# The place of the seventh product between two pairs of column blocks in a hybrid decoder layer

## The chip, the cores and the metric

The kernel runs on one core of one Trainium2 chip. The metric is device time in microseconds (us) for one execution. Three executions of the kernel before took 1405.05, 1405.37 and 1412.27 us; the median is 1405.37 us.

## The reference, cut to what matters

One layer of a decoder with two parallel branches, in float32, on 1024 tokens of width 1024:

```
mod   = silu(c) @ ada_w + ada_b                      # shift, scale, gate
h     = rms_norm(x) * (1 + scale) + shift            # 1024 x 1024
proj  = h @ w_in                                     # 1024 x 11296
gm_u, gm_v, gm_z, ssm_z, xbc, dt_raw, g_a, g_b = split(proj)
y_a   = spatial_gating(gelu(gm_u), gelu(gm_v)) * silu(gm_z)
xbc   = silu(causal_depthwise_conv(xbc))             # 4 taps
y_b   = group_norm((ssd_scan(xbc, dt) + skip) * silu(ssm_z))
merged = sigmoid(g_a) * (y_a @ w_proj_a) + sigmoid(g_b) * (y_b @ w_proj_b)
out   = rms_norm(x + gate * (merged @ w_out))
```

The change concerns `h @ w_in` alone, the widest product.

## The kernel before, in words

Each matrix product is made in float32r from a high and a low part of either operand (high times high, high times low, low times high), and the large ones by a Strassen-Winograd scheme, in which seven products of half-size blocks stand for eight. The stages are: modulation and normalisation (to about 70 us in the profile), the **wide stage** `h @ w_in` (to about 922 us), the state-space scan with `y_a @ w_proj_a` beside it, `y_b @ w_proj_b`, and the output product.

In the wide stage the blocks of `h` stay in on-chip memory. The columns of `w_in` come in blocks of 128, and two blocks make a pair. There are 43 pairs: four of v (v0 to v6), then pairs for the convolution (cb0 to cb7 and x0 to x7) mixed with uz0 to uz7, with z0 to z7 and with seven pairs of gates (g2 to g14). `pair` (L580) makes one pair. Its seven products are called p1, p5, p6, p3, p2, p7 and p4; each is 12 matmuls of 128x512 (`product`, L570). They go to three accumulators in PSUM:

- `px` takes p1. ScalarE copies it to the first half of the tile c1 (L600). Then p6 is added in the same bank, and ScalarE copies the sum to the second half of c1 (L611). Then p7 is added, and VectorE adds px and the saved p5 into the second half of the tile c2 (L622). Last p4 is added, and ScalarE copies px to the first half of c2 (L630).
- `py` takes p5, which ScalarE saves (L606); then p3 is added, and VectorE adds it to c1 (L614).
- `pz` takes p2, which VectorE adds to the first half of c1 (L595).

When c1 is whole, `done1` treats the first block, and after p4 `done2` treats the second: a convolution is one ScalarE pass (L916), three VectorE passes (L918), a SiLU (L920) and a store to DRAM from ScalarE's queue (L93); z and g are one ScalarE pass and a store; u is a GELU, a VectorE product and a store.

The seventh product, p4, isn't made within its own pair. It is put on the list `pending` (L636) and made inside the next pair. Three pairs have nothing pending when they begin, since they are the first or follow a pair made whole: v0, cb0 and g12. The other 40 take over a p4.

What sets the order: TensorE's instructions are pinned (`pin`, which keeps them in the order of the program), and so are the loads on the SP queue. The instructions of ScalarE and VectorE in this stage are mostly not pinned. A scheduler orders them ahead of the run, and gives those issued through `out` (L588) high priority. Each engine then runs its list in order. After each product `run_tasks` (L495) issues the side tasks that have come due; a task's due time counts products.

The tiles c1, c2, the convolution's result ac, the tiles vm and ya of the gating branch, and the short-lived tiles of side tasks (ag and gacc for the output gate, wog for gated weights) all come from one ring of 1024-column tiles, tag w4, with six buffers (`wide`, L164). The writer of a new tile waits until an earlier user of the buffer is done, a store's landing included.

A line in the profile of an instruction issued through `out` is L590, of a matmul in the wide stage L574, of a high part's cast L522. The name `xx<-t4h,p4x2h` tells of a matmul that adds to px of an x pair, here p4 of the pair x2.

Of the kernel before, what the change touches and what calls it, by code (L numbers as in the profile page):

```python
# [35 lines left out]
def hybrid_kernel(  # L36
# [7 lines left out]
    V, A, G, PE = nc.vector, nc.scalar, nc.gpsimd, nc.tensor  # L44
    ctx.enter_context(nc.allow_non_contiguous_dma(reason="small parameter vectors"))

    x, out = x[0], out[0]
# [116 lines left out]
    def wide(name, dt=F32):  # L164
        return w4[0].tile([P, S], dt, name=name, tag="w4", bufs=w4[1])
# [315 lines left out]
    def bank(name):  # L481

        if pairs_done:
            pairs_done.append(name)
            if len(pairs_done) % 4 == 2:
                return psum.tile([P, 512], F32, name=name, tag="px", bufs=2)
        return psum.tile([P, 512], F32, name=name, tag="bk", bufs=6)
# [7 lines left out]
    def run_tasks():  # L495
        slot[0] += 1
        due = [t for t in tasks if t[0] <= slot[0]]
        for t in due:
            tasks.remove(t)
            t[1](*t[2])  # L500
# [69 lines left out]
    def product(ps, l, bn, first=True):  # L570
        (lh, ll), (rh, rl) = l, bop[bn]
        for n, (lw, r) in enumerate(((lh, rh), (lh, rl), (ll, rh))):
            for k in range(4):
                pin(PE.matmul(ps, lw[:, k * P : (k + 1) * P], r[k], start=first and n + k == 0,  # L574
                              stop=n == 2 and k == 3, skip_group_check=not first))
        run_tasks()
# [3 lines left out]
    def pair(name, ops, done1, done2, after=None, whole=False):  # L580

        keep = pin if name in first_c1 and not p2r else lambda i: i
        after = after or (lambda n: None)

        def out(f, *a):  # L588
            with tc.high_priority():
                keep(f(*a))  # L590

        def p2():
            pz = bank(f"z{name}")
            product(pz, ops["p2"], "b21")
            out(V.tensor_add, c1[:, 0:512], c1[:, 0:512], pz)  # L595

        px = psum.tile([P, 512], F32, name=f"x{name}", tag="px", bufs=2)
        product(px, ops["p1"], "b11")
        c1 = first_c1.pop(name) if name in first_c1 else wide(f"c1{name}")
        out(A.copy, c1[:, 0:512], px)  # L600
        after(0)
        py = bank(f"y{name}")
        product(py, ops["p5"], "t1")
        c2 = wide(f"c2{name}") if p2r else None
        p5 = c2[:, 512:1024] if p2r else gm.tile([P, 512], F32, name=f"p5{name}", tag="p5")
        out(A.copy, p5, py)  # L606
        after(1)
        if pending:
            pending.pop()()
        product(px, ops["p6"], "t2", False)  # L610
        out(A.copy, c1[:, 512:1024], px)  # L611
        after(2)
        product(py, ops["p3"], "b22", False)
        out(V.tensor_add, c1[:, 512:1024], c1[:, 512:1024], py)  # L614
        after(3)
        if not whole:
            p2()
            after(4)
            done1(c1)
        product(px, ops["p7"], "t3", False)  # L620
        c2 = c2 or wide(f"c2{name}")
        out(V.tensor_add, c2[:, 512:1024], p5, px)  # L622
        after(4 if whole else 5)
        if whole:
            p2()
            done1(c1)

        def p4():
            product(px, ops["p4"], "t4", False)
            out(A.copy, c2[:, 0:512], px)  # L630
            done2(c2)

        if whole:
            p4()
        else:
            pending.append(p4)  # L636
# [603 lines left out]
    ops = pair_weights(*todo[0][:3], pinned=True)  # L1240
# [4 lines left out]
    for n, (name, _, _, d1, d2, g) in enumerate(todo):  # L1245
# [30 lines left out]
        if n + 1 == len(todo):  # L1276
            pair(name, ops, lambda t: held.append((d1, t)), lambda t: held.append((d2, t)), beside, True)
        else:
            pair(name, ops, d1, d2, ops.get("after"), n in (3, len(jobs) - 1))
        ops = nxt if n else seconds[0]  # L1280
# [532 lines left out]
```

## Time and profile before

| what | us |
|---|---|
| median of three runs | 1405.37 |
| the profiled execution | 1407.67 |
| its span, first to last instruction | 1405.9 |
| TensorE busy in the span | 1377.1 (98%) |
| VectorE busy | 1062.4 (76%) |
| ScalarE busy | 797.0 (57%) |
| GpSimd busy | 213.0 (15%) |
| mean granted TensorE clock | 0.997 of full speed |

Times are from the span's start. In a row of the timeline the first number is the start, the second the length, then come engine, line, operation, tiles, shape and count; brackets at the end tell how long the engine was idle before and what ended the wait.

### The profile page before, as it was taken

To read this page: it belongs to the slowest core of one execution; us is meant where nothing else is said; L and a number is where in the kernel's file an instruction comes from. 1 tells how busy PE (TensorE), PEld (TensorE's weight loads), DVE (VectorE), ACT (ScalarE), POOL (GpSimd) and SP (SyncE) were. 2 spreads that over 40 slices of the span, in tenths; PEclk is the share of its full clock that TensorE was granted. 3 is DMA by queue.
4 is the path that set the end of the run, shared out by engine and by line. 5 is a ranking of instruction groups with operands and counts; after the bars stand their busy time and mean duration, and the time that the engine had idled before them with its cause. 6 is when DMAs were issued, how large, how long until landed. Compare 5 with 4: busy or idle time off the path is not lost.

```text
span 1405.9 us, 20633 instructions
## 1 busy us (share of the span) xinstructions
PE 1377.1 (98%) x7035; PEld 1139.9 (81%) x7035; DVE 1062.4 (76%) x1863; ACT 797.0 (57%) x1471; POOL 213.0 (15%) x208
## 2 busy tenths in 40 slices
PE   8999999999999999999999999999999999999997
PEld 6688888888888888888887888888888877878886
DVE  4786776777778889889788796388667767876976
ACT  5764576556656665556565555677766723322443
POOL 0000000000000011111000010038778740000001
PEclk9999999999999999999999999999999999999999
DMA  8653343343344777787675774598778749878903
GB/s 263 173 165 98 113 120 105 105 121 120 116 125 134 214 202 239 236 248 232 192 221 156 240 214 135 173 353 318 262 253 296 275 168 328 320 231 296 350 33 120
DMA packets 273150, 283.37 MB, mean 202 GB/s; under 512 B 15341, under 2 KB 223637, under 8 KB 273045
## 3 DMA queue, kind: packets, MB, share of 16 engines
q1 hardware_dynamic: 185684, 198.52, 44.4%
q10 hardware_dynamic: 87360, 83.54, 17.8%
q8 instruction: 55, 0.90, 0.3%
q14 instruction: 51, 0.41, 0.1%
HBM read 194.55 MB, written 87.46 MB: 201 GB/s over the span
## 4 chain that ended last, share of the span: by engine, by line
PE 80%; DMA 8%; DVE 5%; POOL 2%; issue 2%; ACT 1%; SPq 1%; ACTq 0%; DVEq 0%; POOLq 0%
PE xcb L574 6%; PE xuz L574 6%; PE xz L574 6%; PE xx L574 5%; PE xg L574 5%; PE x L1477 4%; PE yp L1477 4%; PE ox L1676 3%; PE yuz L574 3%; PE ycb L574 3%; PE pma L81 3%; PE xv L574 3%; PE yz L574 3%; PE yg L574 3%; PE yx L574 3%; DMA dcy<-acs_d 3%
## 5 line engine op out<-in xcount | busy, mean ns | idle before, releaser
L793 POOL TENSOR_TENSOR wog<-wog,gb 128x256 f32<-128x256 f32 x16 | 18.3, 1159 | 676.6 <-PE zz L574 413.3
L1007 ACT ACTIVATE dcy<-dcy,nacs 128x128 f32<-128x128 f32 x256 | 78.6, 388 | 14.9 <-POOL dcy L1002 14.5
L1002 POOL TENSOR_SCALAR_AFFINE_SELECT dcy<-dcy 128x1024 f32<-128x1024 f32 x32 | 35.0, 1095 | 135.7 <-ACT ea L999 132.3
L999 ACT ACTIVATE ea<-dcy 64x512 f32<-64x512 f32 x64 | 40.1, 626 | 14.2 <-DMA dcy<-acs_d 13.8
L920 ACT ACTIVATE ac<-ac 128x1024 f32<-128x1024 f32 x32 | 33.9, 1060 | 23.0 <-DVE ac L918 22.8
L81 PE MATMUL pma<-yh,wah 128*128 128x512 f32 x128 | 43.3, 419 | 0.0
L1027 DVE TENSOR_TENSOR dcy<-dcy,pc 128x1024 f32<-128x1024 f32 x32 | 39.0, 1218 | 4.8 <-PE pc L84 3.0
L81 PE MATMUL pma<-yh,wal 128*128 128x512 f32 x128 | 42.5, 413 | 0.0
L1089 POOL TENSOR_TENSOR yz<-y,sl 128x512 f32<-128x512 f32 x32 | 41.4, 1295 | 1.1
L1087 DVE TENSOR_TENSOR ym<-yn,ea 128x512 f32<-128x512 f32 (+1 forms) x32 | 19.9, 622 | 28.5 <-PE yn L81 28.3
L81 PE MATMUL pma<-yl,wah 128*128 128x512 f32 x128 | 40.1, 394 | 0.0
L1088 POOL TENSOR_TENSOR y<-y,ym 128x512 f32<-128x512 f32 (+1 forms) x32 | 36.6, 1144 | 14.4 <-DVE ym L1087 14.4
L81 PEld LDWEIGHTS yn<-sl,st 128*128 128x128 f32 x224 | 30.3, 190 | 8.3 <-issue 4.4
L81 PE MATMUL yn<-sl,st 128*128 128x128 f32 x224 | 31.6, 276 | 4.9 <-DVE st L1057 4.9
L1416 DVE SCALAR_TENSOR_TENSOR yn<-yn,par,rb 128x512 f32<-128x512 f32 x32 | 24.0, 749 | 15.7 <-DMA yn<-yb_d 15.5
L81 PE MATMUL sp<-xe,bn 128*128 128x256 f32 x112 | 32.6, 408 | 3.3 <-DVE ssq L1117 1.7
L81 PE MATMUL yi<-dcy,xd 128*64 128x128 f32 x512 | 35.7, 283 | 0.0
L918 DVE SCALAR_TENSOR_TENSOR ac<-c2x,cwt,ac 128x1023 f32<-128x1023 f32 (+2 forms) x24 | 31.2, 1300 | 5.3 <-ACT ac L916 5.1
L918 DVE SCALAR_TENSOR_TENSOR ac<-c2cb,cwt,ac 128x1023 f32<-128x1023 f32 (+2 forms) x24 | 31.1, 1296 | 4.4 <-ACT ac L916 4.3
L1691 POOL TENSOR_TENSOR r<-r,fnw 128x512 f32<-128x512 f32 x2 | 2.5, 1296 | 203.7 <-DMA out_dram<-r 203.7
L1055 POOL TENSOR_TENSOR st<-st,cd 128x256 f32<-128x256 f32 x48 | 32.1, 668 | 8.0 <-PE yn L81 5.3
L918 DVE SCALAR_TENSOR_TENSOR ac<-c1cb,cwt,ac 128x1023 f32<-128x1023 f32 (+2 forms) x24 | 31.6, 1318 | 1.3 <-ACT ac L916 1.3
(2980 smaller groups left out, 4390.9 us busy)
## 6 DMA issues: line engine op xcount, KB each, us to landing
sl<-s_d SPq DMA_DIRECT2D x32, 768.0 KB
s_d<-ac ACTq DMA_DIRECT2D x32, 512.0 KB
dcy<-acs_d SPq DMA_DIRECT2D x32, 512.0 KB
aw<-in_ada_w_dram SPq DMA_DIRECT2D x16, 512.0 KB
wbr<-in_w_proj_b_dram SPq DMA_DIRECT2D x64, 128.0 KB
wb_d<-wbb ACTq DMA_DIRECT2D x32, 256.0 KB
wb_d<-wbc ACTq DMA_DIRECT2D x32, 256.0 KB
yb_d<-yz ACTq DMA_DIRECT2D x32, 256.0 KB
```

What stands on the lines that cost most here:

```text
L81: pin(PE.matmul(acc, l, r, start=first, stop=last))
L574: pin(PE.matmul(ps, lw[:, k * P : (k + 1) * P], r[k], start=first and n + k == 0, stop=n == 2 and k == 3, skip_group_check=not first))
L918: V.scalar_tensor_tensor(ac[:, s:], cc[:, : S - s], conv_wt[:, 3 - s, i : i + 1], ac[:, s:], op0=ALU.mult, op1=ALU.add)
L920: A.activation(ac, ac, AF.Silu)
L999: A.activation(ea[hh * HD : (hh + 1) * HD], dcy.rearrange("p (j e) i l -> p e j (i l)", e=2)[hh * HD : (hh + 1) * HD, hh], AF.Exp)
L1002: G.affine_select(out=d8, in_=d8, compare_op=ALU.is_ge, fill=-1e30, base=0, pattern=[[0, 2 * HPG], [1, P]], channel_multiplier=-1)
L1007: A.activation(dcy[:, h, i, :], dcy[:, h, i, :], AF.Exp, bias=sub[:, i, h : h + 1])
L1027: V.tensor_tensor(d3, d3, pc[:, 0:256].unsqueeze(1).to_broadcast([P, HPG, 256]), op=ALU.mult)
L1088: G.tensor_add(y1[:, :, t0:], y1[:, :, t0:], m[:, :, t0:])
L1089: G.tensor_mul(yz, y1, sl[:, 4:6])
L1477: pin(PE.matmul(ps[j], a[:, v, js], r, start=first and n + k == 0, stop=n == 2 and k == KT - 1, skip_group_check=not first))
L1676: pin(PE.matmul(ps, a[:, tsl], b[:, cs], start=first and n + j == 0, stop=n == 2 and j == 3, skip_group_check=not first))
```

## The change

Within a pair, the pending p4 of the pair before was made between p5 and p6. It is now made between p6 and p3.

```
@@ pair
         out(A.copy, p5, py)
         after(1)
+        product(px, ops["p6"], "t2", False)
+        out(A.copy, c1[:, 512:1024], px)
         if pending:
             pending.pop()()
-        product(px, ops["p6"], "t2", False)
-        out(A.copy, c1[:, 512:1024], px)
         after(2)
         product(py, ops["p3"], "b22", False)
```

The order on TensorE was p1, p5, p4 of the pair before, p6, p3, p2, p7; it is p1, p5, p6, p4 of the pair before, p3, p2, p7. In the 40 pairs that take over a p4, one product instead of two stands between p1 and p6, three instead of two between p6 and p7, and three instead of two (counting p1, p5 and p6) between p7 and its own pair's p4. Two stay between p5 and p3. No product, copy, load or store is added or taken away.

More of the change, by code (lines that the diff above doesn't have):

```diff
@@ L607, in pair @@
         after(1)
+        product(px, ops["p6"], "t2", False)
+        out(A.copy, c1[:, 512:1024], px)
         if pending:
             pending.pop()()
-        product(px, ops["p6"], "t2", False)
-        out(A.copy, c1[:, 512:1024], px)
         after(2)
```

## The prediction

> **What bounds the kernel now.** I read the page's first part, then a table by stage (busy time of each engine in chosen windows), then TensorE's waits.
>
> ```profile
> span 1405.9 us, 20633 instructions
> PE 1377.1 (98%) x7035; PEld 1139.9 (81%) x7035; DVE 1062.4 (76%) x1863; ACT 797.0 (57%) x1471; POOL 213.0 (15%) x208
> ```
>
> ```profile
> core 0: us, PE busy (x) PEld busy (x) DVE busy (x) ACT busy (x) POOL busy (x), PEclk, DMA share, GB/s
> 155.00:300.00 145.00, 145.00 (x681) 121.32 (x681) 107.67 (x170) 91.25 (x144) 0.00 (x0) 1.00 0.36 110
> 300.00:480.00 180.00, 180.00 (x828) 150.23 (x827) 138.90 (x186) 111.38 (x174) 0.00 (x0) 1.00 0.46 140
> 480.00:850.00 370.00, 369.26 (x1631) 304.18 (x1630) 316.42 (x592) 214.80 (x366) 30.58 (x24) 1.00 0.72 216
> 1031.25:1034.66 3.41, 3.41 (x25) 3.08 (x25) 2.56 (x4) 1.12 (x4) 2.68 (x3) 0.50 0.88 355
> ```
>
> The first three stretches cover nearly all of the wide stage. TensorE is busy for 694.26 of their 695 us. VectorE is busy 74%, 77% and 86%. So TensorE sets the pace, and two things follow. The change can win next to nothing here, for there is hardly a wait to remove. And whatever makes TensorE wait is added to the end in full, since no other engine is holding the time.
>
> The waits of TensorE in the wide stage that concern p4, p6 and p7 are these (weight loads, PEld, in their own view):
>
> ```profile
> PE xx L574 <- DVE c2x L590: 0.6, 1, 0.6
> ```
>
> ```profile
> PEld xx L574 <- DVE c2x L590: 1.0, 1, 1.0
> PEld xz L574 <- ACT c1z L590: 0.6, 1, 0.6
> PEld xz L574 <- DVE c2z L590: 0.3, 1, 0.3
> ```
>
> **What the change moves.** p6 is added in the bank of p1, so it must wait until ScalarE has copied p1 out. Before, p5 and the foreign p4 ran meanwhile; now p5 alone does. One product is 12 matmuls; from the start of p4 in one row below to the start of p6 in another (750.97 is disturbed, so take 359.47 to 362.19) it lasts 2.72 us. The question is how late the copy is. This is the pair x2, first TensorE, then ScalarE:
>
> ```profile
> 359.47 1.07 PE L574 MATMUL xuz<-t4h,p4uz4h 128*128 128x512 f32 x4
> ...
> 362.19 1.07 PE L574 MATMUL xx<-t2h,p6x2h 128*128 128x512 f32 x4
> ```
>
> ```profile
> 360.45 0.59 ACT L590 COPY c1x<-xx 128x512 f32<-128x512 f32 x1 [1.06 <-DVE gacc L764]
> ```
>
> p6 started at 362.19, long after the copy's end at 361.04, so nobody waited. In the new order p6 wants to start at 359.47, where p4 stands now, and must wait until 361.04. That is how the whole cost is read: **copy's end minus the start of the p4 that follows p5.**
>
> The price of a stop itself is seen where p4 of x6 was held up:
>
> ```profile
> 749.30 1.07 PE L574 MATMUL yz<-t1h,p5z4l 128*128 128x512 f32 x4
> 750.97 1.20 PE L574 MATMUL xx<-t4h,p4x6h 128*128 128x512 f32 x4 [0.60 <-DVE c2x L590]
> ...
> 753.83 1.07 PE L574 MATMUL xz<-t2h,p6z4h 128*128 128x512 f32 x4
> ```
>
> From 750.97 to 753.83 are 2.86 us where an undisturbed product takes 2.72. A restart therefore costs about 0.14 us more, and I add 0.04 us for the signal from ScalarE to TensorE (the delay also seen in the other direction: below, p1 of g12 ends at 885.29 = 884.22 + 1.07, and its copy starts at 885.32). Each stop costs copy's end + 0.18 - p4's start.
>
> In most pairs the copy follows p1 at once. The pair g12, which has no p4 to take over, already has the new order, and shows what happens then:
>
> ```profile
> 884.22 1.07 PE L574 MATMUL xg<-b11h,p1g12l 128*128 128x512 f32 x4
> ...
> 886.94 1.07 PE L574 MATMUL yg<-t1h,p5g12l 128*128 128x512 f32 x4
> 887.85 1.07 PE L574 MATMUL xg<-t2h,p6g12h 128*128 128x512 f32 x4
> ```
>
> ```profile
> 885.32 0.59 ACT L590 COPY c1g<-xg 128x512 f32<-128x512 f32 x1 [1.04 <-PE xg L574]
> ```
>
> The copy is over at 885.91, p6 starts at 887.85 (0.16 us before p5's last row ends at 888.01, the usual overlap), and 1.94 us are to spare. **The new order is free wherever the copy starts less than about 1.9 us after p1's end, and costs wherever it starts later.**
>
> **First term: pairs where the copy is already too late.** I went through ScalarE's timeline pair by pair. In 11 of the 43 pairs the copy ends after the p4 that follows p5 has begun: cb2, x2, x3, x4, cb5, x5, g8, g10, cb7, z5 and x7. The first and the last of them, with x3:
>
> ```profile
> 319.59 1.07 PE L574 MATMUL xuz<-t4h,p4uz3h 128*128 128x512 f32 x4
> ...
> 439.23 1.07 PE L574 MATMUL xuz<-t4h,p4uz6h 128*128 128x512 f32 x4
> ...
> 827.98 1.09 PE L574 MATMUL xz<-t4h,p4z5h 128*128 128x512 f32 x4
> ```
>
> ```profile
> 319.62 0.59 ACT L590 COPY c1cb<-xcb 128x512 f32<-128x512 f32 x1 [1.18 <-DMA s_d<-ac]
> ...
> 439.51 0.59 ACT L590 COPY c1x<-xx 128x512 f32<-128x512 f32 x1 [1.32 <-DMA s_d<-ac]
> ...
> 828.77 0.59 ACT L590 COPY c1x<-xx 128x512 f32<-128x512 f32 x1 [0.45 <-DVE wba L830]
> ```
>
> cb2: 320.21 + 0.18 - 319.59 = 0.80. x2: 361.04 + 0.18 - 359.47 = 1.75. x3: 440.10 + 0.18 - 439.23 = 1.05. x7: 829.36 + 0.18 - 827.98 = 1.56. By the same working the other seven are 0.43, 0.65, 0.46, 0.88, 1.53, 1.68 and 1.05. The 11 sum to **11.8 us**, if each copy keeps its distance from p1.
>
> **Second term: copies that move back.** Several copies are late because c1 has no buffer in the six-deep ring: the brackets name a store's landing (s_d<-ac) or the last reading of another tile of the ring (gacc, whose pass reads ag). The freed buffer is in part the work of the p4 that is moved. For the copy of cb3 the chain can be followed back. TensorE, then ScalarE:
>
> ```profile
> 382.12 1.07 PE L574 MATMUL xx<-t4h,p4x2l 128*128 128x512 f32 x4
> ...
> 399.35 1.07 PE L574 MATMUL xuz<-t4h,p4uz5h 128*128 128x512 f32 x4
> ...
> 420.19 1.07 PE L574 MATMUL xcb<-t4h,p4cb3h 128*128 128x512 f32 x4
> ```
>
> ```profile
> 383.23 0.59 ACT L590 COPY c2x<-xx 128x512 f32<-128x512 f32 x1 [0.28 <-PE xx L574]
> 383.85 1.24 ACT L916 ACTIVATE ac<-c2x,par,cwt 128x1024 f32<-128x1024 f32 x1
> ...
> 387.92 3.19 ACT L882 ACTIVATE vm<-vm,vr 128x128 f32<-128x128 f32 x8 [1.38 <-DMA vm<-v_d]
> ...
> 391.52 1.06 ACT L920 ACTIVATE ac<-ac 128x1024 f32<-128x1024 f32 x1
> ...
> 392.61 0.52 ACTq L93 DMA_DIRECT2D s_d<-ac  x1
> ...
> 397.30 0.59 ACT L590 COPY c1cb<-xcb 128x512 f32<-128x512 f32 x1 [0.75 <-DMA s_d<-ac]
> ...
> 418.58 0.59 ACT L590 COPY c1uz<-xuz 128x512 f32<-128x512 f32 x1 [1.61 <-DVE gacc L764]
> ```
>
> p4 of x2 ends at 383.19, its second convolution begins at once, its store lands, and only then can the copy for cb3 start, 14.1 us later. The new order ends that p4 one product (2.72 us) later against p1 of cb3, and wants p6 one product earlier. The copy of cb3 has 399.35 - 397.89 = 1.46 us to spare now; moved by 2.72 it would cost 2.72 - 1.46 + 0.18 = 1.44.
>
> Five copies between 300 and 480 us wait for such a buffer: cb2, x2, cb3, uz6, x3. For each the move is bounded by 0 below, since SiLUs and stores also stand in line on ScalarE behind other work (the vm passes above, 387.92 to 391.11), which doesn't move, and by 2.72 above. For cb3, whose chain begins at once, I take the whole, 1.44. For the other four I take the middle, 1.36: it adds 1.36 each to cb2, x2 and x3, and uz6 (spare 420.19 - 419.17 = 1.02) comes to 1.36 - 1.02 + 0.18 = 0.52. Together 3 x 1.36 + 1.44 + 0.52 = **6.0 us** (0 to 11.5: 3 x 2.72 + 1.44 + 1.88).
>
> **What else moves.** The moved step issues 12 matmuls, one copy and `done2`, with its ScalarE and VectorE passes and a store on ScalarE's queue; all come one product later, the last of them in the same pair as before, and only a late buffer makes that matter, which is the second term. Side tasks due at the second of the two products are now issued ahead of `done2`; their number, and the order of the loads on the SP queue, stay. GpSimd does nothing in this stage except the gated weights (30.58 us busy of 370); nothing is moved past them. The casts of the next pair's weights keep their places: their buffers are freed one per product, and that count stays.
>
> **What is won.** p4 now has three products behind p7, p7 three behind p6. The three waits quoted above go: x6's p4 (start 750.97 where 750.21 = 750.37 - 0.16 was possible, plus 0.14: 0.9), and the two PEld waits of 0.6 and 0.3, of which the part beyond a normal load and the restart make about 0.4 and 0.2. Together **1.5 us**.
>
> **Sum.** 11.8 + 6.0 - 1.5 = +16.3 us. Against the profiled execution's own time of 1407.67 that is 1424.0; that execution is 2.3 us above the median of the runs shown, 1405.37, so the forecast for the median is 1421.7, say **1422**.
>
> **Rivals.**
>
> 1. *Not slower.* ScalarE's list is drawn up anew, with the copies at high priority. Of the 11 late copies, only cb2, x2 and x3 are held by a buffer by their rows; the other eight (8.2 us) stand behind casts and passes of ScalarE that could come after them. If all eight are drawn forward to p1's end, as in g12, and buffers don't move, there remain 0.80 + 1.75 + 1.05 - 1.5 = +2.1: 1407.5. It decides at a copy that starts 1.9 us after p1's end. For it: ScalarE is busy only 58% from 480 to 850 us. Against it: the copies already had that priority and still came late. Chance 0.20.
> 2. *The ring falls behind everywhere.* 19 copies start more than 0.4 us after p1's end for another reason than TensorE's own work; if all move by the whole 2.72, the stops are 57.2 us by the same sum, and with 1.5 won the time is 1461. Half of that move (1.36) makes 31.4 us of stops, 1435. For it: VectorE is at 86% from 480 us on. Against: a z or g copy can wait for a tile freed by `done1`, which doesn't move, and each stop lets the other engines catch up. Chance 0.18, mostly between 1432 and 1450.
> 3. *The clock falls.* After the longest wait of the scan stage the granted clock is 0.50 for 3.41 us (the fourth row of the table above):
>
> ```profile
> PE yn L81 <- DVE st L1057: 4.9, 5, 2.8
> ```
>
> With the wait of 2.8 us as the point, such a fall costs half of 3.41, 1.7 us. In the forecast only x2 comes near (1.75 + 1.36 = 3.1, less 0.14 of restart and 0.16 of overlap: 2.8 us idle), and I leave its 1.7 out. With the whole 2.72 for the five buffers cb2, x2 and x3 pass it: 11.8 + 11.5 - 1.5 + 3 x 1.7 = +26.9, 1432. Chance 0.10. The Trainium skill, on the page TensorE: Matmul & The Clock Gate, in Part 1 on the HAM clock gate, states that TensorE's clock is halved after about one idle window of 3.4 us, and that the window isn't tied to the kernel. By that rule stops shorter than 3.4 us would leave the sum at +16.3, and only the ones beyond would pay; the trace agrees on the halving and its 3.41 us, but with a wait of 2.8 us ahead of it.
> 4. *Faster by over 0.5%*, 7 us: TensorE's waits here don't add up to that, so only a lucky new order in the later stages could. Chance 0.02.
>
> The forecast's own case (1412 to 1432) has 0.50. A difference of 0.5% is about what a measurement of this kernel can tell from no change. Faster 0.02, within 0.5% 0.20, slower 0.78. The range runs from 1407, in rival 1, to 1442, two thirds of the move in rival 2.
>
> **What would show it.** In the new profile TensorE's waits should name ACT c1cb, c1x, c1z or c1g at L590 ahead of p6, 10 to 16 times, 0.4 to 3 us each; p4 and p7 should wait for nothing; the time after the wide stage should be unchanged, only later. Few such waits would speak for rival 1; such waits in nearly every pair after 300 us for rival 2; a clock below 1.00 in the wide stage for rival 3. The prediction is wrong if the wide stage grows through another wait, on py, or on weights, or if the added time arises after 922 us.

## The result, and the profile after

The changed kernel took 1420.43 us (median of six runs, 1417.38 to 1427.9), the kernel before 1405.94 us on the same occasion (median of six, 1402.67 to 1412.27). The ratio is 1.011, with a 95% interval of 1.009 to 1.0131: about 14.5 us slower. A ratio here and below is worked out from all the executions of both kernels, so it isn't the quotient of the two medians. The forecast was 1422, with a range of 1407 to 1442.

The profiled execution of the changed kernel took 1417.38 us. The first part of its page:

```profile
span 1415.6 us, 20602 instructions
PE 1380.9 (98%) x7035; PEld 1140.8 (81%) x7035; DVE 1060.7 (75%) x1863; ACT 803.3 (57%) x1471; POOL 216.9 (15%) x208
```

TensorE's busy time has hardly grown (1377.1 to 1380.9), while the span grew by 9.7 us. To find the place, I cut the wide stage of each trace into parts at the start of p1 of three pairs: v0 to cb2 ("early"), cb2 to z0 ("middle"), z0 to g12 ("late"). The rows of a window table give the stretch, its length, the busy time of TensorE, its weight loads, VectorE, ScalarE and GpSimd (instructions in brackets), the granted clock, the DMA share and GB/s. First the kernel before:

```profile
70.54:314.15 243.61, 243.54 (x1137) 201.88 (x1136) 178.61 (x315) 147.12 (x235) 1.19 (x1) 1.00 0.39 119
314.15:494.48 180.33, 180.33 (x826) 149.80 (x824) 143.59 (x205) 111.47 (x173) 0.00 (x0) 1.00 0.47 142
494.48:882.40 387.92, 387.18 (x1713) 319.74 (x1712) 320.64 (x588) 221.46 (x373) 30.58 (x24) 1.00 0.69 208
```

Then the changed one, with four short windows that are used below:

```profile
70.77:314.46 243.69, 243.65 (x1137) 201.88 (x1136) 177.99 (x315) 148.81 (x235) 1.43 (x1) 1.00 0.39 119
314.46:503.17 188.71, 182.91 (x826) 150.56 (x825) 143.32 (x204) 112.37 (x174) 0.00 (x0) 0.99 0.44 135
503.17:896.87 393.70, 389.85 (x1714) 320.57 (x1713) 320.80 (x590) 225.56 (x374) 33.60 (x24) 1.00 0.69 205
360.75:364.16 3.41, 0.64 (x3) 0.19 (x1) 2.37 (x3) 1.22 (x3) 0.00 (x0) 1.00 0.78 269
364.16:367.57 3.41, 3.01 (x7) 2.43 (x8) 1.28 (x1) 0.35 (x1) 0.00 (x0) 0.50 0.76 222
780.58:784.00 3.42, 1.31 (x7) 0.77 (x6) 3.42 (x7) 2.59 (x4) 0.00 (x0) 1.00 0.27 90
784.00:787.41 3.41, 3.41 (x10) 2.63 (x9) 3.32 (x8) 2.33 (x5) 0.00 (x0) 0.50 0.62 163
```

The early part is the same (243.61 and 243.69), though ten p4s were moved there. The middle is 8.4 us longer and the late part 5.8 us. With the rest of the stage (39.4 us in both) the wide stage went from 851.2 to 865.5 us: 14.2 us. What TensorE waited for in it:

```profile
PE xx L574 <- ACT c1x L590: 4.3, 4, 3.2
PE xcb L574 <- ACT c1cb L590: 3.3, 3, 1.2
PE xg L574 <- ACT c1g L590: 2.1, 1, 2.1
```

All three rows are matmuls that add to px and wait for a copy into c1, and all are p6. The two longest stops, on TensorE and then on ScalarE:

```profile
364.56 1.65 PE L574 MATMUL xx<-t2h,p6x2h 128*128 128x512 f32 x3 [3.17 <-ACT c1x L590]
...
783.62 1.35 PE L574 MATMUL xg<-t2h,p6g10h 128*128 128x512 f32 x3 [2.11 <-ACT c1g L590]
```

```profile
363.93 0.59 ACT L590 COPY c1x<-xx 128x512 f32<-128x512 f32 x1 [1.91 <-DVE gacc L764]
...
782.99 0.58 ACT L590 COPY c1g<-xg 128x512 f32<-128x512 f32 x1
```

p6 begins 0.04 to 0.05 us after the copy's end (364.52 and 783.57). No p4 and no p7 of the wide stage waits any more.

Counted as the delay of p6 against the usual overlap of 0.16 us, eight pairs stop: cb2 1.29, x2 3.33, x3 0.42, cb4 1.39, cb5 1.07, x5 0.53, x6 0.62 and g10 2.27; with crumbs of under 0.2 us the sum is 11.3. Eight restarts of 0.14 add 1.1. The granted clock was 0.50 twice for 3.41 us, from 364.16 and from 784.00, at the end of the two longest stops. TensorE was busy for 3.01 and 3.41 us of these two windows (rows above), and half of that is lost: 3.2. The waits of p4 and p7 that are gone are worth 1.3. The sum, 11.3 + 1.1 + 3.2 - 1.3 = 14.3, accounts for the 14.2 us.

### The profile page after: what moved, and what is told of

It reads as the page before. It is cut to its first block, busy times and chain, and to the rows that moved or that the text cites. A ratio compares the mean times of both kernels' runs of the same rounds, so it can differ in the third digit from the quotient of the medians.

```text
span 1415.6 us, 20602 instructions
## 1 busy us (share of the span) xinstructions
PE 1380.9 (98%) x7035; PEld 1140.8 (81%) x7035; DVE 1060.7 (75%) x1863; ACT 803.3 (57%) x1471; POOL 216.9 (15%) x208
## 4 chain that ended last, share of the span: by engine, by line
PE 37%; DMA 7%; DVE 4%; POOL 3%; issue 2%; ACT 2%; SPq 1%; ACTq 0%; DVEq 0%; POOLq 0%
PE x L1477 5%; PE xg L574 4%; PE yp L1477 4%; PE xz L574 3%; PE ox L1676 3%; PE pma L81 2%; DMA dcy<-acs_d 2%; PE oy L1676 2%; PE yg L574 2%; DMA yb_d<-yz 2%; PE yz L574 2%; PE xcb L574 2%; PE xx L574 1%; DMA yn<-yb_d 1%; PE zg L574 1%
## 5 line engine op out<-in xcount | busy, mean ns | idle before, releaser
L1007 ACT ACTIVATE dcy<-dcy,nacs 128x128 f32<-128x128 f32 x256 | 78.5, 388 | 16.0 <-POOL dcy L1002 14.5
L999 ACT ACTIVATE ea<-dcy 64x512 f32<-64x512 f32 x64 | 40.1, 627 | 14.2 <-DMA dcy<-acs_d 13.8
```

Of the source, the lines that this page charges most:

```text
L999: A.activation(ea[hh * HD : (hh + 1) * HD], dcy.rearrange("p (j e) i l -> p e j (i l)", e=2)[hh * HD : (hh + 1) * HD, hh], AF.Exp)
L1007: A.activation(dcy[:, h, i, :], dcy[:, h, i, :], AF.Exp, bias=sub[:, i, h : h + 1])
```

## The experiments

Each time of an experiment stands beside runs of the kernel before on the same chip. "Delay" is the delay of p6 (or p4) in the wide stage, counted as above.

**Early pairs only, and late pairs only.** The new order in the first twelve pairs, or in all the others:

```
+        new = name in early          # other kernel: name not in early
+        if pending and not new:
+            pending.pop()()
         product(px, ops["p6"], "t2", False)
         out(A.copy, c1[:, 512:1024], px)
-        if pending:
+        if pending and new:
             pending.pop()()
```

> The new order only in the first twelve pairs (v0 to uz3, ten of them with a pending p4); the other pairs keep the order of before. Theory: a moved p4 costs nothing by itself, only a late copy of p1 does; in these pairs the copy starts 0.04 to 0.14 us after p1's end, so the time is that of before, 1406 within 2 us, and TensorE names no copy of c1 ahead of p6 in them. Rival: each moved p4 costs alike, 14.5 / 40 = 0.36 us, ten of them 3.6 us: about 1409.5.

Measured: 1409.68 us beside 1407.78, ratio 1.0009 (0.9992 to 1.0026): no difference. The early part and the waits of the wide stage:

```profile
71.96:315.67 243.71, 243.65 (x1138) 201.89 (x1136) 178.00 (x315) 148.71 (x234) 1.28 (x1) 1.00 0.39 119
```

```profile
PE xz L574 <- DVE c2z L590: 1.1, 1, 1.1
PE xuz L574 <- DVE c2uz L590: 0.9, 1, 0.9
```

Ten moved p4s cost nothing: the early part took 243.61 us before, and a fixed price would have added 3.6. So the rival of a fixed price falls by the trace; the time alone, whose interval ends at 1.0026 (3.7 us), couldn't exclude it. The two waits belong to p4s in the old order, later in the stage.

> The new order only from the pair cb2 on (30 moved p4s). Theory: all of the loss is here, 1420 within 3 us, with stops ahead of p6 at much the same pairs as in the changed kernel (x2 and g10 the longest). Rival, a like cost for each moved p4: 1406 + 30 x 0.36 = 1417 (the two are hard to tell apart by this run's time alone; its trace tells).

Measured: 1426.56 beside 1407.78, ratio 1.0116 (1.0091 to 1.0141), which by its interval can't be told from that of the whole change (1.011); the median lies above the 1417 to 1423 expected. Middle and late part, and the longest wait:

```profile
314.82:503.73 188.91, 183.47 (x825) 150.57 (x824) 142.87 (x204) 112.07 (x174) 0.00 (x0) 0.99 0.45 135
503.73:896.34 392.61, 388.42 (x1714) 319.40 (x1712) 321.23 (x589) 224.89 (x374) 33.21 (x24) 1.00 0.70 206
```

```profile
PE xx L574 <- ACT c1x L590: 4.6, 4, 3.4
```

The whole loss sits from cb2 on. x2 (3.5 us of delay) and g10 (2.0) are again the longest stops.

**A tile of its own for p1's copy.** c1 takes its buffer of the ring only when p6 is copied:

```
-        c1 = first_c1.pop(name) if name in first_c1 else wide(f"c1{name}")
-        out(A.copy, c1[:, 0:512], px)
+        if name in early:             # cb0 to uz7
+            c1, p1 = None, gx.tile([P, 512], F32, name=f"p1{name}", tag="p1", bufs=2)
+        else:
+            ...
+            p1 = c1[:, 0:512]
+        out(A.copy, p1, px)
...
+        c1 = c1 or wide(f"c1{name}")
         out(A.copy, c1[:, 512:1024], px)
```

> The new order in all pairs, but in the pairs cb0 to uz7 the copy of p1 goes to a tile of its own with two buffers, outside the ring of six; c1 takes its buffer of the ring only at p6's copy, one product later. Theory: the copies of cb2, x2 and x3 are late for want of a buffer of the ring, so their stops vanish (1.29 + 3.33 + 0.42 us of delay, three restarts of 0.14, and one fall of the clock at 364 us of 1.7): about 7 us less than the changed kernel, 1413. Rival: they are late because ScalarE is busy with other work; then the stops stay within half a microsecond and the time is 1420.

Measured: 1420.0 beside 1407.78, ratio 1.0069 (1.0044 to 1.0094). Middle and late part:

```profile
315.09:495.42 180.33, 180.33 (x826) 149.80 (x824) 137.87 (x192) 109.38 (x165) 0.00 (x0) 1.00 0.43 129
495.42:895.10 399.68, 392.19 (x1714) 322.40 (x1713) 325.80 (x600) 225.69 (x378) 36.14 (x24) 0.99 0.70 208
```

In the middle part the result is as clean as can be: 180.33 us, to the hundredth that of before, with TensorE busy throughout. All stops there came from the missing buffer: at cb2, x2 and x3 directly, and at cb4, which kept its tile of the ring, by way of what the pairs ahead of it leave behind. The late part, in which nothing was changed, became 6 us longer than in the changed kernel: the stop at cb5 grew from 1.07 to 3.59 us and the clock was at 0.50 for 6.8 us behind it. So the wide stage fell by 2.4 us (865.5 to 863.1) and not by the 7 expected. The time doesn't show a fall clear of noise: its interval overlaps that of the changed kernel (1.009 to 1.0131), and the median is what the rival expected. It is the trace that refuses the rival. Why the late part grew, with no edit there, no run shows; the likely reason is how the middle part leaves buffers and lists behind.

> The new order; the copy of p1 goes to a tile of its own (one buffer) in all pairs from v2 to z7, outside the ring. To make room, two small tiles of a side task (wba and wbb) share one buffer. Theory: the ring holds up the late copies after 480 us too (cb4, cb5, x5, x6, g10), if indirectly, through the order that the scheduler gave ScalarE; all stops but small ones vanish: 1406 to 1408. Rival: after 480 us ScalarE's own line of work is the reason; the stops there stay (5.9 us of delay, five restarts, one fall of the clock, 8 us in all): 1413 to 1415.

Measured: 1419.4 beside 1407.78, ratio 1.008 (1.0056 to 1.0104). The middle part is 181.28 us, the late part 400.20, with stops at x4, cb5, z2, x5, g10, cb7 and x7. Both expected times are missed, 1406 to 1408 and 1413 to 1415. None of the seven copies waits for its tile by its row, so the ring is not what held them directly. ScalarE ahead of the stop at cb7 (copy of p1 into p1cb):

```profile
800.39 0.41 ACT L830 CAST wbc<-wbr 128x256 fp32r<-128x256 f32 x1 [1.80 <-DVE wbr L850]
800.77 0.40 ACT L830 CAST wbb<-wbr 128x256 fp32r<-128x256 f32 x1
801.09 0.58 ACT L590 COPY p1cb<-xcb 128x512 f32<-128x512 f32 x1
```

ScalarE stood idle for 1.80 us until VectorE had made the side task's sum, and the copy stood behind that cast in ScalarE's list. The theory that the ring holds up the copies after uz7 as well falls. The shared buffer of wba and wbb may have made it worse; this run can't tell.

**The side task's stores on another queue.** In the changed kernel the same shows at cb5, where a store on ScalarE's queue (ACTq) is the obstacle:

```profile
583.26 0.41 ACT L825 CAST wbc<-wbr 128x256 fp32r<-128x256 f32 x1 [2.14 <-DVE wbr L845]
584.80 0.40 ACTq L93 DMA_DIRECT2D wb_d<-wbc  x1
585.24 0.62 ACT L522 CAST p1g4h<-a11g 128x512 fp32r<-128x512 f32 x1 [1.56 <-DVE wbc L830]
585.76 0.58 ACT L590 COPY c1cb<-xcb 128x512 f32<-128x512 f32 x1
```

```
-        store(wb_d[k][:, at : at + n, :, j * P : (j + 1) * P], f32(hl))
+        G.dma_start(wb_d[k][:, at : at + n, :, j * P : (j + 1) * P], f32(hl))
```

> The new order; the stores of the weight side task (wb_d, 96 of them) are issued from GpSimd's queue instead of ScalarE's. Theory for the stops after 480 us: ScalarE's line stands still while such a store waits for VectorE's subtraction, and the copy of p1 stands behind it; freed of that, the stops at cb5, x5, x6 and g10 shrink to under 0.5 us each (from 1.07, 0.53, 0.62 and 2.27 us of delay), while those up to 480 us (cb2, x2, x3) stay: 4 to 6 us less than the changed kernel, about 1415 against a before of 1407. Rival: the ring of six is the reason there too, or ScalarE is merely full; then the stops after 480 us stay within a microsecond in sum.

Measured: 1424.0 beside 1406.64, ratio 1.0119 (1.0096 to 1.0143): no gain in time. Middle and late part:

```profile
314.54:505.98 191.44, 184.50 (x825) 151.36 (x824) 143.93 (x205) 113.28 (x174) 7.58 (x10) 0.98 0.44 134
505.98:895.34 389.36, 387.23 (x1713) 319.68 (x1712) 319.18 (x589) 224.33 (x374) 90.38 (x110) 1.00 0.68 207
```

The late part did what was expected, 389.36 instead of 393.70: x5 and x6 no longer stop, cb5 has 0.63 left, but g10 keeps 1.83. Of the 4.3 us, 1.7 are the clock, which didn't fall behind g10 this time. The copy of g10 stands behind something other than those stores, a pass of the pair z4 that waits for VectorE, and a SiLU (in the changed kernel behind the same pass, at 780.81):

```profile
779.67 1.06 ACT L926 ACTIVATE c1z<-c1z 128x1024 f32<-128x1024 f32 x1 [2.26 <-DVE c1z L590]
...
782.06 1.06 ACT L920 ACTIVATE ac<-ac 128x1024 f32<-128x1024 f32 x1
783.03 0.57 ACT L590 COPY c1g<-xg 128x512 f32<-128x512 f32 x1
```

The middle part took back 2.7 us, with cb4 at 2.06 and the clock at 0.50 for 6.8 us behind x2. The expectation of the time is a miss; that of the stops is met for x5 and x6, nearly for cb5, and not for g10.

**Both, in the new order and in the old.**

> The new order with both causes taken away: the copy of p1 in a tile of its own in the pairs cb0 to uz7, and the side task's stores on GpSimd's queue. Theory (late copies are the whole cost, and these two are why they are late): TensorE's delays ahead of p6 sum to under 3 us (11.3 in the changed kernel), and the time is within 4 us of before. Rival (something else of the new order costs time, or GpSimd's queue delays the side task): over 8 us above before.

Measured: 1410.93 beside 1406.64, ratio 1.0029 (1.0014 to 1.0044); delays 5.0 us (z0, x4, cb5, g10), more than the 3 expected; the time is 4 us above before, at the edge of what was expected.

> Control for the run with both causes taken away: the own tile for p1's copy (cb0 to uz7) and the stores on GpSimd's queue, in the order of before. If the own tile and the queue cost and win nothing by themselves, this is before, 1406 to 1408, with TensorE's delays in the wide stage under 1.5 us, and what the run with the new order had above before (1.0029 times, 4 us) is the price of the new order with its remaining stops (5.05 us of delay, 0.56 of restarts). Rival: the side task on GpSimd's queue costs those 4 us in either order; then this is 1410 to 1412 too.

Measured: 1410.18 beside 1408.23, ratio 1.0011 (0.9998 to 1.0024). The late part, in the new order and then in the old:

```profile
494.73:886.93 392.20, 387.95 (x1714) 319.50 (x1713) 325.75 (x600) 224.72 (x377) 92.38 (x114) 1.00 0.69 212
```

```profile
494.76:886.90 392.14, 388.72 (x1713) 319.14 (x1712) 325.80 (x597) 219.16 (x378) 93.41 (x113) 1.00 0.68 208
```

This is the most telling pair. With the two causes taken away the order of p4 and p6 makes no difference in the wide stage that these two traces show: 855.6 and 855.5 us, both some 4.3 above the 851.2 of before. In the old order the 4.6 us of delay stand ahead of p4, which waits for VectorE's sum into c2; in the new order 5.0 us stand ahead of p6. So the stops are other ones, and that their sums agree this closely may be chance. The control didn't have the under 1.5 us expected; which of its two edits costs that was asked next.

> The order of before, the side task's stores on GpSimd's queue, no own tile. In the control with both, the part of the wide stage from z0 to z7 took 392.1 us against 387.9 before, with stops ahead of p4. If the stores' queue costs that, it is 391 to 393 here too and the time 1.002 to 1.004 times before; if the own tile does (it sets the ring's buffers on another course up to uz7), this part is 388 to 389 here and the time that of before.

Measured: 1407.19 beside 1406.11, ratio 1.0005 (0.9991 to 1.002). The late part:

```profile
494.54:882.57 388.03, 386.95 (x1713) 319.69 (x1712) 318.64 (x589) 220.72 (x373) 93.47 (x110) 1.00 0.68 209
```

388.03 us: the queue costs nothing in the old order, so it is the own tile up to uz7, added to it, that sets the late part on another course, by about 4 us. The own tile without the queue was not run in the old order.

**Work in the two longest stops.** TensorE makes useless matmuls there, whose result nobody reads:

```
+        fill_stop = {"x2": 10, "g10": 6}.get(name, 0)
+        ...
+                pin(PE.matmul(pf, ops["p5"][0][:, 0:P], bop["t1"][0][n % 4], start=True, stop=True))
         product(px, ops["p6"], "t2", False)
```

> The new order, and in the pairs x2 and g10 TensorE makes 10 and 6 more matmuls of 128x512 between p5 and p6 into a bank that nobody reads, 2.3 and 1.4 us, which fit in the idle time that stands there (3.17 and 2.11 us). They add nothing to the result. Theory: TensorE's clock fell twice because those two idle times were long, at a cost of 1.7 us each; kept busy it doesn't fall, and the wide stage is 3.4 us shorter than in the changed kernel (865.5 us), 862. Rival: the idle time has no part in it, the falls stay, the stage is as long or longer.

Measured: 1426.47 beside 1406.64, ratio 1.0146 (1.012 to 1.0171). TensorE at x2:

```profile
361.73 2.43 PE L612 MATMUL fx<-t1h,p5x2h 128*128 128x512 f32 x10
365.09 1.21 PE L574 MATMUL xx<-t2h,p6x2h 128*128 128x512 f32 x4 [0.94 <-ACT c1x L590]
```

The clock didn't fall in the wide stage at all, so the idle time is what lowered it. (It fell at x2 in all five other traces of the new order, or of the stronger dose below, in which the copy of x2 goes to the ring: the changed kernel, the late pairs, the stores on GpSimd's queue, the copy on VectorE and the stronger dose.) But the stage was 867.1 us, not 862: other stops grew (x4 from nothing to 1.63, cb5 from 1.07 to 1.66), and what the clock gave was lost again. The expected time is a miss. The row shows another thing: p6 of x2 starts 294 us after v0 with or without 2.3 us of work ahead of it (365.09 - 71.17 = 293.92; 364.56 - 70.77 = 293.79). The copy there comes at its own time, set by the pass on ag that frees its buffer: in the changed kernel that pass (L764) waits for ag's load to land, starts at 362.61 and takes 1.28 us, and the copy follows at 363.93.

**A stronger dose.** p6 directly behind p1, in all pairs but v0:

```
+        if near:
+            product(px, ops["p6"], "t2", False)
+            out(A.copy, c1[:, 512:1024], px)
         py = bank(f"y{name}")
         product(py, ops["p5"], "t1")
```

> A stronger dose: p6 stands directly behind p1 (all pairs but v0), p5 and the foreign p4 after it. By the formula (copy's end + 0.18 us - start of the next product) even a prompt copy costs 0.04 + 0.59 + 0.18 + 0.16 = 0.97 us, in 42 pairs 41 us, and the pairs with copies up to 4 us late pay up to 2.72 us more each, 13 to 19 such pairs some 30 us: 1406 + 55 to 80 = 1460 to 1485. Rival: if the loss were a fixed price of a moved product, it would be like the changed kernel's, 1420 to 1435.

Measured: 1485.92 beside 1406.64, ratio 1.0564 (1.0533 to 1.0595), just above the upper end. A pair with a prompt copy, TensorE and ScalarE:

```profile
637.81 1.07 PE L574 MATMUL xg<-b11h,p1g4l 128*128 128x512 f32 x4
639.55 1.19 PE L574 MATMUL xg<-t2h,p6g4h 128*128 128x512 f32 x4 [0.68 <-ACT c1g L590]
```

```profile
638.91 0.58 ACT L590 COPY c1g<-xg 128x512 f32<-128x512 f32 x1 [0.28 <-PE xg L574]
```

p1 ends at 638.88, p6 would have begun 0.16 earlier and begins at 639.55: 0.83 of delay and 0.14 of restart, the 0.97 of the formula. It recurs as 0.835 or 0.836 us in 20 pairs. The formula of the prediction holds for them. The total is no proof of it: the granted clock was 0.50 in seven windows of this wide stage, which cost 9.8 us (half of TensorE's busy time in them), and the expectation had nothing for that.

**The copy on VectorE.**

```
-        out(A.copy, c1[:, 0:512], px)
+        out(V.tensor_copy, c1[:, 0:512], px)
```

> The new order, the copy of p1 made by VectorE instead of ScalarE in all pairs. If ScalarE's line is the reason after 480 us, the stops at cb5, x5, x6 and g10 shrink (3.9 to 4.5 us of delay in the kernels so far become under 2), while cb2, x2 and x3 stay late for want of a buffer: about 3 us less than the changed kernel, 1.009 times before. If the lines are late on either engine alike (VectorE is 86% busy there and waits in order too), the delays stay at 10 to 13 us and the time at 1.011 to 1.015 times before.

Measured: 1446.32 beside 1408.23, ratio 1.0274 (1.0253 to 1.0294); delays 29.0 us. Both expectations missed, on the dear side. The largest two groups of waits:

```profile
PE xcb L574 <- DVE c1cb L590: 10.1, 4, 5.1
PE xx L574 <- DVE c1x L590: 5.1, 3, 3.3
```

The granted clock was 0.50 in five windows of the wide stage, 8.1 us more. The middle part grew to 205.1 us; the likely reason, which no run tested, is that a copy that waits for a buffer now holds up VectorE's list, in which passes that free buffers stand. After 480 us x5 vanished and g10 fell to 0.37, but cb5 stayed at 1.04, x6 grew to 1.63, and z4 came new with 2.76. It doesn't settle which list is late.

**The kernel before once more.**

> The kernel before once more, for a second trace. The stages behind the wide stage took 484.2 us in its first trace and 479.4 in that of the changed kernel. Theory: that is scatter between executions and no doing of the change; this trace has 484.2 only by chance and may lie anywhere from 479 to 488, while the wide stage is 851.2 within 0.5 us. Rival: the new order shortens the later stages; then it is 484 within 1.

Measured: one run, 1406.59 us; wide stage 852.3 us, 1.1 more than in the first trace and outside the 0.5 expected, since p4 of x6 waited 1.4 us instead of 0.6; the stages behind it 1404.9 - 925.2 = 479.7 (484.2 in the first trace). Over all kernels here they took 479 to 488 us whatever the order. So the 4.8 us by which the changed kernel's trace is shorter there are scatter; the medians don't have them.

This trace shows more. ScalarE takes its instructions of the wide stage in the order of the first trace, and yet the copies of p1 don't keep their places: those of z5 and x7 started 2.86 and 3.35 us after p1's end in the first trace, 0.67 and 1.84 us in the second. The working of the prediction's first term, on the second trace, gives nine late pairs in place of 11, without z5 and x7, and 10.9 us.

## Why the prediction was right, and where its sizes were off

- **What bounds the kernel.** Right. TensorE was busy through the stage, and what stops it is added to the end: 14.2 us in the stage, 14.5 between the medians.
- **The price rule** (copy's end + 0.18 - start of the next product). Right, shown by the stronger dose at 0.97 us for a prompt copy, and by the early pairs at nothing.
- **First term, late copies that keep their distance from p1: 11.8.** Too large, and mostly after 480 us. There eight pairs were to cost 8.2 us; x4, g8, cb7, z5 and x7 didn't stop, cb5, x5, x6 and g10 did, 4.5 us of delay, 5.1 with restarts. The step that failed is that each copy keeps its place. In that part the copy stands in ScalarE's list behind casts, passes and stores that wait for VectorE, and the list was drawn up anew. At cb7, where p1 ended at 787.23 before and at 801.83 after, a cast of the side task went from behind p4's cast to ahead of it. ScalarE before, then after:

```profile
786.70 0.60 ACT L522 CAST p4cb7h<-a22cb 128x512 fp32r<-128x512 f32 x1
...
788.20 0.41 ACT L825 CAST wbc<-wbr 128x256 fp32r<-128x256 f32 x1 [0.89 <-DVE wbr L845]
...
790.72 0.58 ACT L590 COPY c1cb<-xcb 128x512 f32<-128x512 f32 x1
```

```profile
799.81 0.41 ACT L825 CAST wbc<-wbr 128x256 fp32r<-128x256 f32 x1 [1.22 <-DVE wbr L845]
...
801.11 0.61 ACT L522 CAST p4cb7h<-a22cb 128x512 fp32r<-128x512 f32 x1
...
802.57 0.58 ACT L590 COPY c1cb<-xcb 128x512 f32<-128x512 f32 x1
```

  The copy came 3.49 us after p1's end before, and 0.74 after. At cb5 and x5 the order is the same in both, and only the waits differ. And z5 and x7, 2.6 of the 8.2 us, were late in the first trace of before and not, or just not enough, in the second: one execution was too little to read them from.
- **Second term, copies that move back: 6.0.** Right that the middle part suffers from the ring of six (the own tile removes all of it, 8.4 us, 1.5 of them the clock), wrong in the pairs. cb3 was to wait for the store of the moved p4's work; it started 0.45 us after p1's end. Its buffer came from another tile, c1 of the pair uz5, freed by a VectorE product:

```profile
403.85 0.59 ACT L590 COPY c1cb<-xcb 128x512 f32<-128x512 f32 x1 [0.70 <-DVE ya L902]
```

  The prediction followed one buffer; in the changed kernel the copy got another. With both terms, and restarts counted, cb3 (1.44 forecast) and uz6 (0.52) cost nothing, cb2 1.43 (2.16 forecast) and x3 0.56 (2.41); cb4 (0 forecast) cost 1.53 and x2 3.47 (3.11). So in the middle part the stops were 7.0 where the two terms had 9.6. Over the whole stage the two terms were 17.8, the stops measured 12.4.
- **What is won: 1.5.** Right, 1.3; no p4 and no p7 waits. In the second trace of before these delays come to 2.1 us, so this term varies from execution to execution.
- **The clock** was a rival with 0.10 and left out of the sum. It came true in part and cost 3.2 us, at one stop above the assumed 2.8 us (3.17) and at one below it (2.11). It made up for much of what the two terms had too much.
- **Rival 1**, that the copies of the late part are drawn forward, came true in part: five pairs of eight didn't stop, of which g8 and cb7 came 1.15 us and more earlier than in either trace of before, x4 by 0.15 us, and z5 and x7 are open as said; rival 2 didn't come.

So the mechanism, the place and the sign were right, and the number was good because terms too large by 5.4 us met one of 3.2 that had been left out; that part was luck. What stays open: which share of the late part's stops is ScalarE's list and which the ring. The stores' queue alone takes 4.3 of the 5.8 us away there, 1.7 of them the clock, but the list changes with every edit, and no run held it still.

## What to carry to other kernels

Before moving work that stands between a copy and the next use of its accumulator, look up in the trace how late that copy is in every round, not in a typical one: the work between is a cushion, and here 2.72 us of it were too few for eight copies out of forty. Ask of a late copy whether its source, its target's buffer or its engine's list is late; a tile of its own cured the second at once and did nothing for the third. Look at more than one execution: two of the eleven late copies were not late enough in the next trace of the same kernel. And a cushion taken from one wait (p6) goes to others (p4, p7): where those had 1.3 us to win in all, there was nothing to move it for.

## What the runs showed of the hardware

In these traces the granted clock falls by the idle share of a fixed window. The falls of one execution lie at whole multiples of 3.413 us from each other, so the windows can be laid out. In the changed kernel the windows ahead of the two falls had TensorE busy for 0.64 and 1.31 of 3.41 us (rows above): 81% and 62% idle. Over the wide stages of this study all 18 windows with 59% idle or more were followed by a low clock, and no fall began after one with 52% or less; none lay between (a second low window can follow a first at 31% or 41%). The two that lie nearest to the line, of the own tile up to uz7 (59%, a fall) and of the late pairs only (52%, none):

```profile
576.92:580.34 3.42, 1.40 (x7) 0.82 (x5) 3.20 (x5) 0.41 (x1) 1.52 (x1) 1.00 0.87 255
```

```profile
781.52:784.93 3.41, 1.64 (x7) 1.39 (x8) 3.41 (x7) 2.22 (x5) 0.00 (x0) 1.00 0.46 154
```

In the scan stage, with its many small matmuls, the line is less sharp: three windows of 55% or 56% were not followed by a fall, one of 55% was, and one of 39% was. An example without a fall is this window of the run with both causes taken away (TensorE busy 1.69, 50% idle, a stop of 1.7 us):

```profile
577.20:580.61 3.41, 1.69 (x8) 1.10 (x7) 3.41 (x9) 3.04 (x7) 0.97 (x2) 1.00 0.50 159
```

So a stop of 2.1 us lowered the clock where it lay within one window (g10 in the changed kernel), and one of 2.32 us that the grid cuts in two did nothing (cb0 in the stronger dose, from 161.30 to 163.62 us, cut at 162.38). The prediction had set the point at 2.8 us. The Trainium skill, on the page TensorE: Matmul & The Clock Gate, Part 1, has the same window of about 3.4 us, not tied to the kernel's start, but asks for at least one idle window. Here a window that was 59% idle was enough, and the measurement decides.
